# Start of a transformer-block kernel: the first loads spread over three queues, and the warming products on another operand

## The chip, the cores and the metric

The kernel runs on one core of one Trainium2 chip. The metric is the device time of one execution in microseconds (us). The kernel before took 763.39 us, the median of three runs that lie between 763.17 and 763.40 us. A core has five engines that run side by side and wait for each other through semaphores: TensorE (PE, with the weight loads as a track of their own, PEld), VectorE (DVE), ScalarE (ACT), GpSimd (POOL) and SyncE (SP). Transfers are issued from the queues of SP, ScalarE or GpSimd and carried by 16 DMA engines.

## The reference

One block of 512 positions and 1024 features: a gated linear attention and a latent attention in parallel, merged, then a squared-ReLU feed-forward, all in float32.

```python
def rmsnorm(x, g):
    xf = x.astype(jnp.float32)
    y = xf * lax.rsqrt(jnp.mean(xf * xf, axis=-1, keepdims=True) + EPS)
    return (y * g.astype(jnp.float32)).astype(x.dtype)

def reference(x, positions, g_mix, w_in, ...):
    h = x
    for l in range(DEPTH):
        n = rmsnorm(h, g_mix[l])
        proj = n @ w_in[l]
        (gq, gk, gv, gr, z_gf, z_gb, cq, ckv, kr, z_ma, z_mb) = jnp.split(proj, SPLIT_IDX, axis=-1)
        y_gla = gla_branch(gq, gk, gv, gr, z_gf, z_gb, ...)
        y_mla = mla_branch(cq, ckv, kr, positions, ...)
        merged = jax.nn.sigmoid(z_ma) * y_gla + jax.nn.sigmoid(z_mb) * y_mla
        h = h + merged @ w_out[l]
        m = rmsnorm(h, g_mlp[l])
        h = h + jnp.square(jax.nn.relu(m @ w_ff1[l])) @ w_ff2[l]
    return rmsnorm(h, g_final)
```

What matters here is the first line of the loop and the beginning of the second: x times the norm's factors g_mix, and its product with the first 512 columns that the kernel uses of w_in.

## The kernel before

Features lie on the 128 partitions and positions in the free dimension, so x comes transposed ("xt") in eight tiles of 128 features by 512 positions, xraw[0] to xraw[7] (256 KB each; called x in the profile). The first four blocks of output features that are projected have their weights gathered in "w_first", eight tiles of 128 by 512, vraw[0] to vraw[7] (256 KB each; vw in the profile). The factors of all norms, the biases and a few constants come in one array "columns" of 128 rows of 39 words, which lands in gvec; gmix is the part of it for the first norm.

A float32 product is made of three products of a narrower type: every operand is split into a high half (rounded) and a low half (the rest), and high times high, low times high and high times low are added up in one accumulator. So each tile costs ScalarE an activation for the high half and VectorE a subtraction for the low half before TensorE can use it. For x the high half carries the factors too (split_scaled, lines 97 and 98: ScalarE multiplies by gmix and rounds, VectorE multiplies and subtracts the rounded half). For the weights split does it (lines 93 and 94), except for the first tile: there VectorE makes the high half by a copy (line 341, CAST in the profile) and the low half by a subtraction (line 343). VectorE's order for this first tile is: high half of the weights, low half of x, low half of the weights.

first_with(k) (line 327) makes the twelve products of tile k: four accumulators f_accs (called first) by three pairs of halves, in the order high by high, low weights by high x, high weights by low x. In the profile the halves of the first two weight tiles are first0h and first0l, those of the next two first1h and first1l, and so on; xT is x's pair of halves.

What happens at the start, with the lines that the change and the prediction speak of:

- GpSimd builds ident (the unit matrix, by make_identity in masks.py), after (line 137 and 138), ones (line 142) and the small constants half_pi and mhalf. ident is used later for transposing and for diagonals (line 289), mhalf as the exponent of the reciprocal roots (line 279).
- VectorE copies ones into ones_r (line 144), the operand with which a diagonal is spread over the partitions (line 298).
- ScalarE loads its function table (line 150) and issues the transfer of gvec on its own queue (line 155).
- SP's queue issues x[0], vw[0], x[1], vw[1] and so on (lines 311 and 312), then the weights of later stages, in the order of the program. A transfer that reuses one of eight semaphores waits on the queue until the earlier transfer of that semaphore has landed.
- TensorE makes eight warming products ident times ident into an accumulator that nobody reads (line 317; 16 records in the profile, two passes for each product), and then the products of line 327.

The order of the work on each engine from line 315 on is the order of the program: in_program_order(fixed) adds a dependency without a semaphore from each instruction to the next of its engine. goes_behind(late, early, engines) does the same for one pair: the first instruction of `late` on an engine comes after the last one of `early` there. Lines further down (from line 355) multiply xraw by gmix in place, sum the squares, and project the next blocks (zb2, zb3), whose weights are transferred by begin_late (line 238).

```python
for k in range(KD):
    nc.sync.dma_start(xraw[k], t["xt"][k * P : (k + 1) * P, :])
    nc.sync.dma_start(vraw[k], t["w_first"][k * P : (k + 1) * P, :])
...
for _ in range(8):
    nc.tensor.matmul(warm[:, :P], ident, ident, start=True, stop=True)
```

Of the kernel before, what the change touches and what calls it, by code (L numbers as in the profile page):

```python
# [11 lines left out]
F32 = mybir.dt.float32  # L12
# [6 lines left out]
P = 128  # L19
# [37 lines left out]
def tile_block(ctx: ExitStack, tc: tile.TileContext, t, out: bass.AP):  # L57
    nc = tc.nc
# [9 lines left out]
    def u2(name, dt=F32, shape=(P, S)):  # L68
        return tl(list(shape), dt, "u2", 29, name)
# [7 lines left out]
    def ps(tag, name):  # L77
        serial[0] += 1
        return pp.tile([P, S], F32, tag=tag, bufs=4, name=f"{name}_{serial[0]}")

    def one(shape, dt, name):
        return sb.tile(shape, dt, tag=name, bufs=1, name=name)

    def raw(x):
        return x.bitcast(F32)
# [14 lines left out]
    def issued_after(ins, before):  # L100
        tc.add_manual_dep(
            ins, before,
            mybir.DependencyInfo(mybir.DependencyClass.NoSync, mybir.DependencyReason.DATA),
            reason="program order",
        )

    def traced():
        return len(nc.cur_bb.bb.instructions)
# [12 lines left out]
    SP_ONLY = (mybir.EngineType.SP,)  # L121
# [3 lines left out]
    def goes_behind(late, early, engines):  # L125

        ins = nc.cur_bb.bb.instructions
        for e in engines:
            a, b = [[i for i in ins[x:y] if i.engine == e] for x, y in (early, late)]
            if a and b:  # L130
                issued_after(b[0], a[-1].name)


    ident = one([P, P], F32, "ident")
    make_identity(nc, ident)
    after = one([P, P], F32, "after")
# [2 lines left out]
        after, after, pattern=[[-1, P]], compare_op=ALU.is_gt, fill=0.0, base=0, channel_multiplier=1  # L139
    )  # L140
    ones = one([P, P], F32, "ones")
    nc.gpsimd.memset(ones, 1.0)
    ones_r = one([P, P], F32R, "ones_r")
    nc.vector.tensor_copy(ones_r, ones)
    half_pi = one([P, 1], F32, "half_pi")
# [4 lines left out]
    nc.scalar.preload_act_table_set("exp_and_others")  # L150


    V_GLA, V_Q, V_KV, V_MLP, V_BF, V_BB, V_MIX, V_CST = 0, 8, 11, 13, 21, 25, 29, 37
    gvec = one([P, 48], F32, "gvec")
    nc.scalar.dma_start(gvec[:, 0 : V_CST + 2], t["columns"])
    gmix, cst = gvec[:, V_MIX : V_MIX + 8], gvec[:, V_CST : V_CST + 2]

    gates = {}
# [52 lines left out]
    def stage(nk, nw, name):  # L211
        wf = tl([P, nk, nw], F32, "wf", 3, f"{name}f")
        return wf

    def halves(nk, nw, name):
        wh = tl([P, nk, nw], F32R, "wh", 4, f"{name}h")
        wl = tl([P, nk, nw], F32R, "wl", 4, f"{name}l")
        return wh, wl
# [16 lines left out]
    def begin_late(col, name, tag="mm", w=None):  # L235

        wf = stage(KD, P, name)
        nc.sync.dma_start(wf, (w_in if w is None else w)[:, col : col + P].rearrange("(k p) w -> p k w", p=P))
        wh, wl = halves(KD, P, name)
        nc.scalar.activation(wh, wf, AF.Copy)  # L240

        def lows():
            nc.vector.tensor_tensor(wl, wf, raw(wh), op=ALU.subtract)

        return (wh, wl, ps(tag, name)), lows
# [20 lines left out]
    def feature_sums(sq, name, tag="at"):  # L266
        tot = ps(tag, f"{name}ss")
        for j in range(NT):
            nc.tensor.matmul(tot[:, j : j + 1], sq[:, j * P : (j + 1) * P], ones[:, 0:1], start=True, stop=True)
        return tot  # L270
# [36 lines left out]
    xraw = [u2(f"x{k}") for k in range(KD)]  # L307
    vraw = [u2(f"vw{k}") for k in range(KD)]

    for k in range(KD):  # L310
        nc.sync.dma_start(xraw[k], t["xt"][k * P : (k + 1) * P, :])
        nc.sync.dma_start(vraw[k], t["w_first"][k * P : (k + 1) * P, :])

    fixed = traced()
    warm = ps("at", "warm")
    for _ in range(8):
        nc.tensor.matmul(warm[:, :P], ident, ident, start=True, stop=True)
    f_accs = [ps("mm", f"first{i}") for i in range(NT)]
    vh = [halves(2, S, f"first{k}") for k in range(KD // 2)]
    sq = None  # L320
# [10 lines left out]
    def add_square(k, before):  # L331
        q = u2(f"sq{k}")
        nc.scalar.activation(q, xraw[k], AF.Square)
        if before is not None:
            nc.vector.tensor_tensor(q, q, before, op=ALU.add)
        return q
# [13 lines left out]
            sq = add_square(k - 1, sq)  # L350
    sq = add_square(KD - 1, sq)
    x_tot = feature_sums(sq, "x")
    zb_early = [begin_late(C_ZB + f * P, f"zb{f}", tag) for f, tag in ((2, "at"), (3, "mm"))]
    for k in range(KD):
        nc.scalar.activation(xraw[k], xraw[k], AF.Copy, scale=gmix[:, k : k + 1])
    first_with(6)
# [756 lines left out]
    for n, (a, m) in enumerate(steps[:-4]):  # L1113
# [4 lines left out]
        if steps[n + 1] in fillers:  # L1118
            at = traced()
# [113 lines left out]
    at = traced()  # L1233
# [8 lines left out]
    at = traced()  # L1242
# [8 lines left out]
    at = traced()  # L1251
# [12 lines left out]
    for n in range(4 * MH + LAG_C - 1):  # L1264
# [43 lines left out]
        if n == 17:  # L1308
            at = traced()
# [246 lines left out]
    at = traced()  # L1556
# [9 lines left out]
    at = traced()  # L1566
# [7 lines left out]
    at = traced()  # L1574
# [12 lines left out]
    at = traced()  # L1587
# [55 lines left out]
def build(arrays):  # L1643
    nc = bacc.Bacc("TRN2", target_bir_lowering=False, num_devices=1, dynamic_dma_scratch_size=8192)
    t = {
        n: nc.dram_tensor(f"in_{n}", list(a.shape), mybir.dt.from_np(a.dtype), kind="ExternalInput").ap()
        for n, a in arrays.items()
    }
    out = nc.dram_tensor("out_0", [1, S, D], F32, kind="ExternalOutput").ap()
    with tile.TileContext(nc) as tc:  # L1650
        tile_block(tc, t, out)
    return nc
# [16 lines left out]
```

## Time and profile before

| | before |
|---|---|
| median of 3 runs | 763.39 us |
| all runs | 763.39, 763.17, 763.40 us |
| the profiled execution's own time | 762.79 us |
| its span, first to last instruction | 761.0 us |
| mean granted TensorE clock | 0.999 |
| transfers | 81.28 MB, mean 107 GB/s |

The profile shows one execution. Its page gives busy time and share for each engine, the span in 40 slices, the transfers, and the chain of work that ended last, followed back from the end. The other views are answers from the same trace: a timeline (start, duration, engine with the line of the source, operation, output<-inputs, shapes, count, and in brackets the idle time of the engine before the instruction and what ended it), busy times in windows, and the instructions of one tile or one line. "x<-in_xt" is a transfer into a tile x from the input xt. SPq, ACTq and POOL mark the queue that issues a transfer; the time beside it is that of issuing, and the time to landing is shown apart. Times start at the first instruction of the span. The end of a matmul is modelled, so that the start of one is the better mark.

### The profile page before, as it was taken

Reading aid. Unit: us, or ns where it says so; the run is one execution under the profiler, and the core shown is the slowest. Engines: PE = TensorE matmul, PEld = TensorE weight load, DVE = VectorE, ACT = ScalarE, POOL = GpSimd, SP = SyncE. Lnnn points to the kernel's source line nnn. Section 1 sums busy time; section 2 is a strip of 40 time slices with the busy share of each in tenths; the row PEclk is TensorE's granted clock in tenths of the full one; section 3 lists DMA queues with packets and bytes.
Section 4 is the critical chain, followed back from the end, with each engine's and each line's share of the span. In section 5 each row is a group of like instructions: output and inputs, shape, how many; then the busy total and the mean of one; then the engine's idle time right before and its main releaser. Section 6 shows DMA issues by size and latency. Waiting matters only on the chain.

```text
span 761.0 us, 10233 instructions
## 1 busy us (share of the span) xinstructions
PE 752.1 (99%) x3744; PEld 636.1 (84%) x3744; DVE 580.7 (76%) x850; ACT 453.3 (60%) x768; POOL 150.5 (20%) x226
## 2 busy tenths in 40 slices
PE   9999999999999999999999999999999999999996
PEld 7888788888898889898888988888888888888885
DVE  7779999756767775998897786955796578748795
ACT  8456668475466555888866675435553555345644
POOL 0710005260615104127761100000000000000014
PEclk9999999999999999999999999999999999999999
DMA  9843310221324416127988421362116410650002
GB/s 312 255 112 108 93 28 28 56 59 54 84 60 112 82 33 155 25 71 191 272 189 229 140 80 56 111 196 80 55 56 195 137 42 15 195 165 1 28 1 110
DMA packets 97185, 81.28 MB, mean 107 GB/s; under 512 B 15504, under 2 KB 74896, under 8 KB 97136
## 3 DMA queue, kind: packets, MB, share of 16 engines
q1 hardware_dynamic: 93904, 74.33, 33.3%
q0 software_dynamic: 2944, 6.03, 4.3%
q8 instruction: 29, 0.48, 0.3%
q10 hardware_dynamic: 288, 0.28, 0.1%
q14 instruction: 20, 0.16, 0.1%
HBM read 76.96 MB, written 2.10 MB: 104 GB/s over the span
## 4 chain that ended last, share of the span: by engine, by line
PE 97%; DVE 1%; ACT 1%; issue 0%; POOL 0%; POOLq 0%; ACTq 0%
PE f L88 8%; PE f L89 8%; PE f L90 8%; PE gx L88 4%; PE gx L90 4%; PE gx L89 4%; PE first L327 3%; PE tp L1042 2%; PE za L88 2%; PE za L89 2%; PE za L90 2%; PE gz L88 2%; PE gz L90 2%; PE gz L89 2%; PE zb L88 1%; PE zb L90 1%
## 5 line engine op out<-in xcount | busy, mean ns | idle before, releaser
L1608 POOL DMA_DIRECT2D gfin<-in_g_final x1 | 0.6, 622 | 284.0 <-PE f L90 284.0
L914 DVE TENSOR_TENSOR w<-w,w 128x1024 f32<-128x1024 f32 x32 | 38.7, 1221 | 0.3
L475 POOL COPY v3f<-rrf 128x4 f32<-128x4 f32 x4 | 2.8, 708 | 135.9 <-DVE rrf L458 135.9
L1027 ACT ACTIVATE e<-s,top 128x512 f32<-128x512 f32 x32 | 21.9, 685 | 4.8 <-DVE top L1022 3.9
L94 DVE TENSOR_TENSOR pT<-tp,pT 128x512 fp32r<-128x512 f32 x32 | 21.7, 682 | 2.9 <-ACT pT L93 2.9
L1022 DVE TENSOR_REDUCE top<-s 128x1 f32<-128x512 f32 x32 | 21.6, 681 | 2.0 <-PE s L90 1.7
L1335 DVE TENSOR_TENSOR h<-h,gx 128x512 f32<-128x512 f32 x32 | 21.5, 682 | 1.9 <-PE gx L90 1.8
L93 ACT ACTIVATE pT<-tp 128x512 fp32r<-128x512 f32 x32 | 18.8, 593 | 4.2 <-PE tp L1042 3.9
L1042 PE MATMUL tp<-ident,e 128*128 128x128 f32 x128 | 19.3, 274 | 0.4 <-ACT e L1033 0.2
L88 PE MATMUL av<-pT,v 128*128 128x256 f32 x64 | 19.0, 297 | 0.0
L93 ACT ACTIVATE ghb<-y 128x512 fp32r<-128x512 f32 x16 | 10.1, 632 | 14.0 <-DVE y L860 14.0
L1401 ACT ACTIVATE fa<-f 128x512 f32<-128x512 f32 x32 | 18.5, 577 | 0.0
L89 PE MATMUL av<-pT,v 128*128 128x256 f32 x64 | 18.2, 285 | 0.0
L1042 PEld LDWEIGHTS tp<-ident,e 128*128 128x128 f32 x128 | 15.1, 140 | 3.7 <-ACT e L1033 1.0
L94 DVE TENSOR_TENSOR sc<-sc,sc 128x512 fp32r<-128x512 f32 x16 | 10.9, 691 | 9.5 <-ACT sc L93 9.5
L90 PE MATMUL av<-pT,v 128*128 128x256 f32 x64 | 18.1, 283 | 0.0
L93 ACT ACTIVATE sc<-sc 128x512 fp32r<-128x512 f32 x16 | 9.3, 596 | 11.5 <-DVE sc L546 11.5
L93 ACT ACTIVATE b_00h<-w 128x1024 fp32r<-128x1024 f32 x7 | 7.4, 1061 | 12.6 <-PE gx L90 6.0
L93 ACT ACTIVATE b_20h<-w 128x1024 fp32r<-128x1024 f32 x7 | 7.4, 1061 | 12.1 <-PE gx L90 6.0
L93 ACT ACTIVATE b_10h<-w 128x1024 fp32r<-128x1024 f32 x7 | 7.4, 1061 | 12.1 <-PE gx L90 6.0
L88 PE MATMUL s<-kbuf,q 96*128 96x512 f32 x32 | 14.1, 440 | 0.0
L1410 ACT ACTIVATE px<-fa 128x256 f32<-128x256 f32 x32 | 13.4, 418 | 1.0
(1667 smaller groups left out, 2927.9 us busy)
## 6 DMA issues: line engine op xcount, KB each, us to landing
w<-in_w_ff SPq DMA_DIRECT2D x64, 256.0 KB, 3.5
w<-in_w_out POOLq DMA_DIRECT2D x10, 512.0 KB, 9.4
grw<-in_w_in SPq DMA_DIRECT2D x8, 512.0 KB, 8.5
gvw<-in_w_in SPq DMA_DIRECT2D x8, 512.0 KB, 4.6
w<-in_w_out SPq DMA_DIRECT2D x16, 256.0 KB, 5.8
x<-in_xt SPq DMA_DIRECT2D x8, 256.0 KB, 5.2
vw<-in_w_first SPq DMA_DIRECT2D x8, 256.0 KB, 5.3
h<-in_x SPq DMA_DIRECT2D x4, 512.0 KB, 5.0
```

What stands on the lines that cost most here:

```text
L88: nc.tensor.matmul(acc, lh, rh, start=start, stop=False, skip_group_check=onto)
L89: nc.tensor.matmul(acc, lh, rl, start=False, stop=False, skip_group_check=onto)
L90: nc.tensor.matmul(acc, ll, rh, start=False, stop=stop, skip_group_check=onto)
L93: nc.scalar.activation(hi, src, AF.Copy)
L94: rest.tensor_tensor(lo, src, raw(hi), op=ALU.subtract)
L327: nc.tensor.matmul(f_accs[i], a[:, i * P : (i + 1) * P], b, start=k == 0 and x == 0, stop=k == KD - 1 and x == 2)
L914: nc.vector.tensor_tensor(wq[dst][g], wq[x][g], wq[y][g], op=op)
L1022: nc.vector.tensor_reduce(top, acc, axis=AX.X, op=ALU.max, negate=True)
L1027: nc.scalar.activation(e, acc, AF.Exp, bias=top, accum_out=tot[:, qt % 2 : qt % 2 + 1])
L1042: nc.tensor.transpose(tp[:, k * P : (k + 1) * P], e[:, k * P : (k + 1) * P], ident)
L1335: nc.vector.tensor_tensor(hc, hc, acc, op=op)
L1401: nc.scalar.activation(a, acc, AF.Relu)
```

## The change

Four things at the start of the program are changed; nothing is added to or taken from the computation.

1. The transfer of gvec moves from ScalarE's queue to GpSimd's and stands ahead of everything else there.
2. The transfer of the first weight tile, vw[0], moves from SP's queue to ScalarE's. The other weight tiles and all of x stay on SP's.
3. ones is filled by VectorE in place of GpSimd, and the eight warming products take ones for both operands in place of ident.
4. The transfers of zb2 and zb3 are tied behind those of x and w_first on SP's queue by goes_behind.

```diff
+    V_GLA, V_Q, V_KV, V_MLP, V_BF, V_BB, V_MIX, V_CST = 0, 8, 11, 13, 21, 25, 29, 37
+    gvec = one([P, 48], F32, "gvec")
+    nc.gpsimd.dma_start(gvec[:, 0 : V_CST + 2], t["columns"])
     ident = one([P, P], F32, "ident")
     make_identity(nc, ident)
...
     ones = one([P, P], F32, "ones")
-    nc.gpsimd.memset(ones, 1.0)
+    nc.vector.memset(ones, 1.0)
     ones_r = one([P, P], F32R, "ones_r")
     nc.vector.tensor_copy(ones_r, ones)
...
-    V_GLA, V_Q, V_KV, V_MLP, V_BF, V_BB, V_MIX, V_CST = 0, 8, 11, 13, 21, 25, 29, 37
-    gvec = one([P, 48], F32, "gvec")
-    nc.scalar.dma_start(gvec[:, 0 : V_CST + 2], t["columns"])
     gmix, cst = gvec[:, V_MIX : V_MIX + 8], gvec[:, V_CST : V_CST + 2]
...
+    landing = traced()
     for k in range(KD):
         nc.sync.dma_start(xraw[k], t["xt"][k * P : (k + 1) * P, :])
-        nc.sync.dma_start(vraw[k], t["w_first"][k * P : (k + 1) * P, :])
-
+        (nc.sync if k else nc.scalar).dma_start(vraw[k], t["w_first"][k * P : (k + 1) * P, :])
+
+    landing = landing, traced()
     fixed = traced()
     warm = ps("at", "warm")
     for _ in range(8):
-        nc.tensor.matmul(warm[:, :P], ident, ident, start=True, stop=True)
+        nc.tensor.matmul(warm[:, :P], ones, ones, start=True, stop=True)
...
     x_tot = feature_sums(sq, "x")
+    at = traced()
     zb_early = [begin_late(C_ZB + f * P, f"zb{f}", tag) for f, tag in ((2, "at"), (3, "mm"))]
+    goes_behind((at, traced()), landing, SP_ONLY)
```

In the program as built, the order on each engine is the one of before except for these: VectorE begins with the memset of ones and the copy into ones_r (before, that copy stood after the low half of the second weight tile), GpSimd begins with the transfer and no longer fills ones, and SP's queue has one transfer less, so that x[1] follows x[0] there. zb2 and zb3 stood behind x and w_first before, too.

## The prediction

> **What bounds the kernel now.** I read the page's shares first, then the chain of work that ended last, then the first microseconds by timeline, windows and tiles, because every edit lies there.
>
> ```profile
> span 761.0 us, 10233 instructions
> PE 752.1 (99%) x3744; PEld 636.1 (84%) x3744; DVE 580.7 (76%) x850; ACT 453.3 (60%) x768; POOL 150.5 (20%) x226
> 1.53 3.50 PE warm L317 x16
> 5.03 0.96 PE first L327 x4
> 6.01 15.71 PE first L327 x68
> ```
>
> TensorE is busy 752.1 of 761.0 us. The chain starts with the warming products and goes straight into the first projections; from 6.01 on they run without a gap (68 products in 15.71 us, 0.231 each). So the moment at which TensorE enters that unbroken run carries to the end one for one, and nothing earlier counts. What sets 6.01 is in the timeline (start, duration, engine, work, then the idle time before it and what ended that):
>
> ```profile
> 0.80 0.39 SPq L311 DMA_DIRECT2D x<-in_xt  x1
> 0.82 0.39 ACTq L155 DMA_DIRECT2D gvec<-in_columns  x1
> 1.18 0.29 POOL masks.py:199 TENSOR_SCALAR_AFFINE_SELECT ident<-ident 128x128 f32<-128x128 f32 x1
> 1.24 0.42 SPq L312 DMA_DIRECT2D vw<-in_w_first  x1
> 1.53 3.31 PEld L317 LDWEIGHTS warm<-ident 128*128 128x128 f32 x16 [1.53 <-POOL ident masks.py:199]
> 1.68 0.20 POOL L142 MEMSET ones<- 128x128 f32 x1
> 1.70 0.43 SPq L311 DMA_DIRECT2D x<-in_xt  x1
> 3.84 0.72 ACT L97 ACTIVATE xT<-x,gvec 128x512 fp32r<-128x512 f32 x1 [1.77 <-DMA gvec<-in_columns]
> 4.26 0.43 DVE L341 CAST first0h<-vw 128x512 fp32r<-128x512 f32 x1 [4.26 <-DMA vw<-in_w_first]
> 4.60 0.75 DVE L98 SCALAR_TENSOR_TENSOR xT<-x,gvec,xT 128x512 fp32r<-128x512 f32 x1
> 4.80 0.75 PEld L327 LDWEIGHTS first<-xT,first0h 128*128 128x128 f32 x4
> 5.27 0.68 DVE L343 TENSOR_TENSOR first0l<-vw,first0h 128x512 fp32r<-128x512 f32 x1
> 5.64 0.72 ACT L97 ACTIVATE xT<-x,gvec 128x512 fp32r<-128x512 f32 x1 [1.07 <-DMA x<-in_xt]
> 6.00 0.76 PEld L327 LDWEIGHTS first<-xT,first0l 128*128 128x128 f32 x4 [0.46 <-DVE first0l L343]
> 6.28 0.63 ACT L93 ACTIVATE first0h<-vw 128x512 fp32r<-128x512 f32 x1
> 7.07 0.69 DVE L94 TENSOR_TENSOR first0l<-vw,first0h 128x512 fp32r<-128x512 f32 x1
> 7.67 0.22 DVE L144 CAST ones_r<-ones 128x128 fp32r<-128x128 f32 x1
> ```
>
> Read backwards: the second group of products (6.00) waits 0.46 us for the low half of the first weights (DVE, 5.27 to 5.95). That follows on VectorE the low half of x (4.60 to 5.35), and that has two predecessors which end together. One is ScalarE's high half of x, 3.84 to 4.56, waiting for the norms' factors; the other is VectorE's own cast of the first weights, which waits for their tile and starts at 4.26, so that the next instruction follows 0.34 later. Thus
>
> low half of x starts = the later of (ScalarE start + 0.76) and (cast start + 0.34): 4.60 and 4.60,
>
> and TensorE's unbroken run starts 1.40 later. Both arms are tight: a gain needs both earlier, a loss needs only one later. The warming products are a third arm for the first group alone (4.80), which is followed by the 0.46 us gap and so has that much slack.
>
> How long the transfers take from issue to landing (views by line or by tile: the issue's row, then minimum, median and maximum of that row's transfers):
>
> ```profile
> L155 ACTq DMA_DIRECT2D gvec<-in_columns x1: 394/394/394, 0.8 to 0.8; - x1
> DMA to landing us min/median/max: 2.9/2.9/2.9
> L311 SPq DMA_DIRECT2D x<-in_xt x3: 388/432/432, 0.8 to 2.7; - x3
> DMA to landing us min/median/max: 2.7/3.9/4.3
> L312 SPq DMA_DIRECT2D vw<-in_w_first x2: 416/424/433, 1.2 to 2.2; - x2
> DMA to landing us min/median/max: 3.0/3.5/4.1
> L1129 POOL DMA_DIRECT2D pos_i<-in_positions x1: 772/772/772, 41.0 to 41.0; - x1
> DMA to landing us min/median/max: 3.8/3.8/3.8
> ```
>
> The shortest x is the first (an empty queue): it lands at 0.80 + 2.7 = 3.5. The first weight tile lands at 1.24 + 3.0 = 4.2, the factors at 0.82 + 2.9 = 3.7, which is 0.1 before ScalarE starts. The last pair of rows is GpSimd's first transfer today, 256 KB, at 41 us.
>
> **The change, part by part.** The order of instructions on each engine stays the same but for the moved ones.
>
> *First weight tile on ScalarE's queue.* Issued at 0.82 in place of 1.24, so at best it lands at 0.82 + 2.7 (the first x) = 3.5, 0.7 earlier; at worst at 4.2 as now. Which, the windows say (length, busy times, granted clock, DMA share, GB/s):
>
> ```profile
> 1.50:2.00 0.50, 0.47 (x2) 0.47 (x3) 0.00 (x0) 0.50 (x1) 0.50 (x6) 1.00 0.87 61
> 2.00:2.50 0.50, 0.50 (x4) 0.50 (x4) 0.00 (x0) 0.07 (x1) 0.02 (x1) 1.00 0.36 124
> 2.50:3.00 0.50, 0.50 (x5) 0.50 (x4) 0.00 (x0) 0.00 (x0) 0.00 (x0) 1.00 1.04 371
> 3.00:3.50 0.50, 0.50 (x4) 0.50 (x4) 0.00 (x0) 0.00 (x0) 0.00 (x0) 1.00 1.06 385
> 3.50:4.00 0.50, 0.50 (x4) 0.50 (x4) 0.00 (x0) 0.16 (x1) 0.00 (x0) 1.00 1.14 324
> ```
>
> From 2.5 us on the transfer engines are full. In the first two windows they move 31 + 62 = 93 KB, then 186 and 193 KB. The first x (262 KB) and the factors (20 KB, 128 rows of 39 words) make 282 KB, done at 3.0; with the weight tile 544 KB, done at 3.7. Each lands about 0.5 later, which fits 3.5 and 4.2. Nothing is idle that an earlier issue could use, except before 2.5. If the weight tile's packets take turns with x from 2.5 on, x has some 170 KB left and gets half of 380 GB/s: done 0.9 later, at 3.4, landing at 3.9 instead of 3.5. Bounds: x lands at 3.5 (it keeps its place) to 4.2 (both end together); the weights at 3.5 to 4.2. I take 3.9 for x and 4.1 for the weights, since a second queue's transfer (the factors today) already lands beside the first x and not behind the transfers queued on SP. The second x is issued 0.46 earlier (at 1.24), but the bytes ahead of it are the same 512 KB, so ScalarE's second high half stays near 5.64. It may be late by some 0.9: it ends, with its weights, at 6.28 + 0.63 = 6.91, and TensorE needs it only after twelve products, 6.0 + 8 x 0.231 = 7.8.
>
> The Trainium skill ("DMA: Bandwidth & Descriptors", section "Issuing engines are not separate DMA queues") says that transfers issued from several engines interleave on the same 16 DMA engines and that only issue time is saved. By it the sum's gain would be at most the 0.42 us of issue time in the weights' arm, while x pays for the interleaving; the full windows above agree with it.
>
> *Factors on GpSimd.* Issued at about 0.79, before its first memset. Bounds for the landing: 2.9 as on ScalarE's queue (3.7), and 3.8 as for the positions (4.6). The positions carry 256 KB, which at 380 GB/s is 0.7 us; without them 3.1, or 3.9. But they landed on idle engines, and the factors have to take turns with two streams where they now have one. I take the middle of the bounds, 4.1. GpSimd's other start work is delayed by the issue, 0.77 as for the positions. Its cover is in these rows (the power reads mhalf, the diagonal reads ident), ident, for one, is written at 1.18:
>
> ```profile
> 22.86 1.89 POOL L279 TENSOR_TENSOR r_x<-r_x,mhalf 128x4 f32<-128x4 f32 x1 [20.84 <-DVE r_x L278]
> 25.60 1.23 DVE L289 TENSOR_TENSOR xdg<-ident,xrh 128x512 fp32r<-128x512 f32 x1
> ```
>
> Without that cover it would cost its 0.77.
>
> *Warming operand on VectorE.* VectorE stands idle until 4.26, so the memset (0.20 on GpSimd; on VectorE between half and twice the 0.22 of the cast, which has the same shape) and the cast, moved from 7.67, are free there. The warming products start at about 0.79 + 0.20 + 0.06 = 1.05, 0.48 earlier, and are through by about 4.3. They did not set 6.00, so this gives nothing; the removed 0.22 at 7.67 lies in VectorE's slack (the second tile's low weights, just ahead of it, are ready at 7.76 and needed after 7.8 + 4 products = 8.7). Order constraints on the SP queue: nothing.
>
> *Sum.* ScalarE starts at 4.1 + 0.1 = 4.2 (factors; x at 3.9 is earlier), the low half of x at 4.2 + 0.76 = 4.96 (weights' arm 4.1 + 0.37 = 4.47), against 4.60: +0.35. Between the two estimates of the landing, 3.9 and 4.1, it is +0.15 to +0.35; I round to +0.3. Profiled execution: 762.79 = span 761.0 + 1.8 around it, so 763.1; the median of the runs, 763.39, lies 0.6 above the profiled one, so 763.7. Bounds: all at the early ends gives ScalarE at 3.6 or 3.8, so -0.2 to 0; the factors at 4.6 give +0.9.
>
> **Rivals.**
>
> *It does what it says* (25%). The factors land as before or earlier, x keeps its place, the weights gain 0.4. For it: GpSimd has nothing before the issue, and 20 KB is little. Against it: the full windows. ScalarE at 3.6 to 3.8: 763.2 to 763.4.
>
> *The factors come much too late* (5%; slower). One transfer from GpSimd, made under full queues, behaves like its later ones beside SP's stream:
>
> ```profile
> L910 POOL DMA_DIRECT2D w<-in_w_out x10: 1181/1248/1692, 355.7 to 400.5; - x10
> DMA to landing us min/median/max: 5.9/9.4/12.6
> ```
>
> Even the quickest of them, 5.9, puts the landing at 6.7 and ScalarE at 6.8, 3.0 later: 766.4. It decides from a landing at 5.3 (4.5 after the issue), where the loss passes 1.5 us. Against it: those move 512 KB each and add to what lies there; the positions took 3.8.
>
> *The clock is late* (3%; slower).
>
> ```profile
> L317 PEld LDWEIGHTS warm<-ident x16: 192/333/333, 1.5 to 4.6; 128*128 128x128 f32 x16
> ```
>
> The warming loads run at 333 ns and the last at 192, some 3.1 us after the first: TensorE comes to speed just as the products begin. If the earlier warming ends at 4.3, TensorE rests until 5.2, and another 3.1 us from 4.3 has to pass, the products up to 7.4 take twice as long: half of 2.2, 1.1, with the 0.3 above 764.8. Against it: warming starts earlier too and should reach speed by 4.2. The Trainium skill ("TensorE: Matmul & The Clock Gate", section "What's actually happening") has free-running windows of 3413 ns, by which the step could also come up to a window later; no run here shows that.
>
> **How the numbers follow.** The forecast (+0.1 to +0.9, mostly by the factors or x) holds 67%, the gain 25%, late factors 5%, late clock 3%. What a measurement of this kernel can tell from no change is about 0.2%, 1.5 us. The gain and the forecast both lie within it; beyond it on the slow side lie late factors and a small part of the rest, 6%; on the fast side there is no room, since both arms end in transfers that cannot land before 3.5, so 1%. The range is 763.0 (the gain, with the spread of the runs) to 764.5 (factors at 4.6 and 0.2 of spread).
>
> **What would show it.** In the changed profile ScalarE's first high half should start at 4.0 to 4.4 and name gvec or x as its releaser, the first cast at or a little before 4.2, the warming products near 1.05, and TensorE's second group near 6.3 after a gap on the low weights. The forecast is wrong if ScalarE starts before 3.84, if the second group starts before 6.0, if TensorE has a new gap between 6.3 and 30 us, or if the clock step comes after the first products.

## The result, and the profile after

| | before | after |
|---|---|---|
| median of 7 runs on one chip | 763.40 us (762.90 to 764.05) | 766.38 us (765.53 to 766.65) |
| ratio, 95% interval | | 1.0035 (1.0023 to 1.0047) |
| the profiled execution's own time | 762.79 us | 765.86 us |
| its span | 761.0 us | 764.1 us |

The change makes the kernel 2.98 us slower by the medians (1.8 to 3.6 by the interval), which is outside the predicted range and more than the 0.2% that a measurement of this kernel can tell from no change. The page of the changed kernel still has TensorE as the bound, busy 99% of a span that is 3.1 us longer. 1.9 of these 3.1 us are more busy time (754.0 against 752.1), and that is the first hint that waiting alone does not explain the loss (a product at a slow clock is busy for longer):

```profile
span 764.1 us, 10232 instructions
PE 754.0 (99%) x3744; PEld 637.5 (83%) x3744; DVE 580.7 (76%) x851; ACT 453.1 (59%) x768; POOL 151.1 (20%) x226
```

The chain of waits after no longer begins with the warming products. Its first links (start, duration, work) are the factors' transfer, ScalarE's high half of x, and then TensorE without a gap:

```profile
1.33 4.31 DMA gvec<-in_columns
5.67 0.73 ACT xT L97
6.44 17.97 PE first L329 x72
```

The timeline after, in the columns of the timeline before:

```profile
0.82 0.40 ACTq L313 DMA_DIRECT2D vw<-in_w_first  x1
1.11 3.49 PEld L319 LDWEIGHTS warm<-ones 128*128 128x128 f32 x16 [1.11 <-DVE ones L145]
1.33 0.76 POOL L136 DMA_DIRECT2D gvec<-in_columns  x1 [0.83 <-POOLq L1648]
4.76 0.43 DVE L343 CAST first0h<-vw 128x512 fp32r<-128x512 f32 x1 [3.44 <-DMA vw<-in_w_first]
5.67 1.33 ACT L97 ACTIVATE xT<-x,gvec 128x512 fp32r<-128x512 f32 x2 [3.59 <-DMA gvec<-in_columns]
6.42 0.75 DVE L98 SCALAR_TENSOR_TENSOR xT<-x,gvec,xT 128x512 fp32r<-128x512 f32 x1 [1.23 <-ACT xT L97]
6.44 1.35 PEld L329 LDWEIGHTS first<-xT,first0h 128*128 128x128 f32 x4 [1.84 <-ACT xT L97]
7.89 1.57 PEld L329 LDWEIGHTS first<-xT,first0l 128*128 128x128 f32 x4
9.49 1.79 PEld L329 LDWEIGHTS first<-xT,first0h 128*128 128x128 f32 x8
```

Beside it, the third group of products in the timeline before:

```profile
6.80 1.80 PEld L327 LDWEIGHTS first<-xT,first0h 128*128 128x128 f32 x8
```

Read the starts one after the other. ScalarE begins 1.83 us late (5.67 against 3.84), because the factors were issued at 1.33 and took 4.3 us. TensorE's second group is 1.89 late (7.89 against 6.00). The third group is 2.69 late (9.49 against 6.80): another 0.80 was lost between the second and the third group, where TensorE waits for nobody. The durations say why. Four loads of the first group take 1.35 us where they took 0.75, and those of the second 1.57 where they took 0.76: these eight products ran at the slow pace of the warming. The record of TensorE's granted clock that each trace keeps (no view prints its events) says the same: the clock goes up to full at 9.36 us, in the trace before at 4.60. After that the two traces run in step. The gate's activations, one row of each kernel's view by tile (minimum, median and maximum duration in ns, first and last start), are 2.7 and 2.6 us apart; before:

```profile
L442 ACT ACTIVATE l<-gatef,gvec x4: 682/684/692, 111.1 to 216.6; 128x512 f32<-128x512 f32 x4
```

and after:

```profile
L446 ACT ACTIVATE l<-gatef,gvec x4: 683/684/691, 113.8 to 219.2; 128x512 f32<-128x512 f32 x4
```

The remaining 0.4 us of the span (3.1 less 2.69) come somewhere later. Executions of the kernel before differ by more than that among themselves, so it is not pursued. The account is 1.8 us for late factors, 0.8 us for slow first products.

Issue and landing after, by tile (the issue's row, then minimum, median and maximum from issue to landing; for a line with several issues the first is the shortest):

```profile
L136 POOL DMA_DIRECT2D gvec<-in_columns x1: 757/757/757, 1.3 to 1.3; - x1
DMA to landing us min/median/max: 4.3/4.3/4.3
L312 SPq DMA_DIRECT2D x<-in_xt x8: 328/393/519, 0.8 to 8.5; - x8
DMA to landing us min/median/max: 3.8/5.3/5.7
L319 PEld LDWEIGHTS warm<-ones x16: 288/333/337, 1.1 to 4.3; 128*128 128x128 f32 x16
```

The first x lands at 0.80 + 3.8 = 4.6 and the weight tile just before its cast, at 4.7. Both are later than the prediction's worst case of 4.2, only the factors are later still. The last row shows that the warming never came to speed: none of its sixteen loads took less than 288 ns, where the last one before took 192.

### The profile page after: what moved, and what is told of

Read it like the earlier page. It is cut to its first block, busy times and chain, and to the rows that moved or that the text cites. A ratio compares the mean times of both kernels' runs of the same rounds, so it can differ in the third digit from the quotient of the medians.

```text
span 764.1 us, 10232 instructions
## 1 busy us (share of the span) xinstructions
PE 754.0 (99%) x3744; PEld 637.5 (83%) x3744; DVE 580.7 (76%) x851; ACT 453.1 (59%) x768; POOL 151.1 (20%) x226
## 4 chain that ended last, share of the span: by engine, by line
PE 96%; DVE 1%; ACT 1%; DMA 1%; issue 0%; POOL 0%; POOLq 0%; ACTq 0%
PE f L88 8%; PE f L90 8%; PE f L89 8%; PE gx L88 4%; PE gx L89 4%; PE gx L90 4%; PE first L329 3%; PE tp L1046 2%; PE za L88 2%; PE za L89 2%; PE za L90 2%; PE gz L90 2%; PE gz L88 2%; PE gz L89 2%; PE zb L88 1%; PE zb L89 1%
```

## The experiments

The question was which of the moved pieces costs the 1.8 us, whether the 0.8 us is TensorE's clock, and why 20 KB take 4.3 us from GpSimd. The kernel before ran on the same chip beside each: its median was 763.60 us beside the first four experiments, 763.40 beside the held stream, the two repeats and the last kernel of all, and 763.44 beside the others. Ratios are to these.

**Factors back on ScalarE's queue, ahead of the weight tile.** Taken from the changed kernel:

```diff
-    nc.gpsimd.dma_start(gvec[:, 0 : V_CST + 2], t["columns"])
+    nc.scalar.dma_start(gvec[:, 0 : V_CST + 2], t["columns"])
```

> The changed kernel with the factors back on ScalarE's queue, ahead of the first weight tile there; SP carries x and the other weight tiles as in the change. Theory 'GpSimd's path': the factors land near 3.9, and only the smaller loss from the two queues taking turns stays: x lands near 4.5, ScalarE starts near 4.6 (3.84 before, 5.67 changed), the time is 0.8 to 1.2 us over before, 1.8 to 2.2 us under the change. Rival 'two queues' (the interleaving of x and the first weight tile is the whole cause, and delayed the factors too): ScalarE starts above 5.2 and the time stays within 0.7 us of the change. Rival 'nothing but GpSimd': ScalarE starts by 3.9 and the time is that of before.

Measured: median 766.12 us, ratio 1.0027 (1.0016 to 1.0039), with six runs in two groups: 764.23 and 764.57, and four from 765.79 to 766.56. The profile is that of the 764.23. Its timeline:

```profile
1.26 0.43 ACTq L313 DMA_DIRECT2D vw<-in_w_first  x1
3.89 0.72 ACT L97 ACTIVATE xT<-x,gvec 128x512 fp32r<-128x512 f32 x1 [1.38 <-DMA gvec<-in_columns]
5.05 0.43 DVE L343 CAST first0h<-vw 128x512 fp32r<-128x512 f32 x1 [3.73 <-DMA vw<-in_w_first]
6.80 0.76 PEld L329 LDWEIGHTS first<-xT,first0l 128*128 128x128 f32 x4 [0.44 <-DVE first0l L345]
7.61 1.79 PEld L329 LDWEIGHTS first<-xT,first0h 128*128 128x128 f32 x8
```

ScalarE is back at 3.89, so the 1.8 us by which it was late belonged to the factors. But the weights' arm is now late. Their tile, issued at 1.26 (1.24 before), lands 3.8 later (3.0 before), the cast starts at 5.05 instead of 4.26, and the third group is 0.81 late. This is about the expected size for an execution whose products run at speed, but not at the expected place: x was to land near 4.5, and it landed at 3.7, while the weights were late. The median missed it, and why there are two groups was left to later runs, below.

**Weight tile back on SP's queue, factors still on GpSimd.**

```diff
-        (nc.sync if k else nc.scalar).dma_start(vraw[k], t["w_first"][k * P : (k + 1) * P, :])
+        nc.sync.dma_start(vraw[k], t["w_first"][k * P : (k + 1) * P, :])
```

> The changed kernel with the first weight tile back on SP's queue; the factors stay on GpSimd as its first work. Theory 'GpSimd's path': the factors are issued near 1.33 and land at 5.2 to 5.7, though x lands near 3.5 again; ScalarE starts at 5.3 to 5.7 and the time is 1.5 to 3 us over before. Rival 'two queues': with one queue at the start the factors land within 3 us of their issue, by 4.3, ScalarE starts by 4.4 and the time is at most 0.6 us over before.

Measured: median 766.39, ratio 1.0034 (1.0021 to 1.0046), the whole loss of the change. The timeline has the cast early again and the factors as late as ever:

```profile
4.13 0.43 DVE L343 CAST first0h<-vw 128x512 fp32r<-128x512 f32 x1 [2.82 <-DMA vw<-in_w_first]
5.78 1.34 ACT L97 ACTIVATE xT<-x,gvec 128x512 fp32r<-128x512 f32 x2 [3.71 <-DMA gvec<-in_columns]
```

The two queues are not needed for the loss; the factors from GpSimd are enough. The weight tile's move is enough for most of it too, by the median of the first experiment: 766.12 with that move alone, 766.39 with the factors' alone, 766.38 with both. The two losses do not add up; the part on the clock, below, gives a reading of why.

**The warming operand alone,** on the kernel before: ones filled by VectorE, the warming products on ones.

```diff
-    nc.gpsimd.memset(ones, 1.0)
+    nc.vector.memset(ones, 1.0)
...
-        nc.tensor.matmul(warm[:, :P], ident, ident, start=True, stop=True)
+        nc.tensor.matmul(warm[:, :P], ones, ones, start=True, stop=True)
```

> The kernel before with ones filled by VectorE and the warming products on ones; all transfers as before. Theory: ScalarE still starts near 3.84 and TensorE's second group near 6.0; warming runs from 1.1 to 4.5 to 4.9 and there is no gap ahead of the first products, so the time is that of before within 0.4 us. Rival 'clock': the earlier warming ends before TensorE's speed comes up, the first products' weight loads run at 333 ns in place of 188, and the time is 0.8 us or more over before.

Measured: median 763.64, ratio 1.0001 (0.9992 to 1.0010). This part costs nothing that can be measured. Against this kernel, the second experiment's differs in the queue of the factors (and in part 4 of the change, which left the order on SP's queue as it was): 763.64 and 766.39 beside the same kernel before.

**Twice the warming,** on the changed kernel, so that TensorE works until the late first products come:

```diff
-    for _ in range(8):
+    for _ in range(16):
```

> The changed kernel with sixteen warming products in place of eight. Theory: the gap of 1.55 us ahead of the first products goes, the weight loads of the first eight products run at 188 ns in place of 333, TensorE's third group starts 0.7 to 0.9 us earlier (near 8.7), and the time is 0.5 to 1.0 us under the change; the rest of the loss, about 2 us over before, stays because ScalarE still starts near 5.6. If the slow first products had another cause than the gap, nothing changes, or the longer warming itself delays the first products (later than 6.5).

Measured: median 765.11, ratio 1.0022 (1.0013 to 1.0031). Timeline:

```profile
1.11 5.01 PEld L319 LDWEIGHTS warm<-ones 128*128 128x128 f32 x32 [1.11 <-DVE ones L145]
5.52 1.33 ACT L97 ACTIVATE xT<-x,gvec 128x512 fp32r<-128x512 f32 x2 [3.45 <-DMA gvec<-in_columns]
6.29 0.76 PEld L329 LDWEIGHTS first<-xT,first0h 128*128 128x128 f32 x4 [0.17 <-ACT xT L97]
7.68 0.75 PEld L329 LDWEIGHTS first<-xT,first0l 128*128 128x128 f32 x4 [0.63 <-DVE first0l L345]
8.48 1.81 PEld L329 LDWEIGHTS first<-xT,first0h 128*128 128x128 f32 x8
```

Here all products run at speed (four loads in 0.76 and 0.75), and the third group comes at 8.48 instead of 9.49. ScalarE was 0.15 earlier here, so 0.8 to 0.9 of that is the slow pace taken away. What stays over before is 1.68 us in the trace (8.48 less 6.80) and 1.51 by the medians, less than the 2 that were expected: the factors' share. That the longer warming is what took the slow pace away is not shown by this one trace, since its clock goes up at 4.01 us, which eight products would have reached as well. The times speak for it: seven of the ten lie from 764.93 to 765.23, under all twelve of the two kernels with late factors and eight warming products (765.41 to 766.79).

**Where GpSimd's time goes: a spare transfer late in the kernel.** On the kernel before, 8 KB that nobody reads, once while SP streams weights and once right behind the positions, when SP's queue moves nothing (gvec's tile is narrowed to make room):

```diff
+    spare = one([P, 16], F32, "spare")
+    nc.gpsimd.dma_start(spare, t["columns"][:, 0:16])
...
+            nc.gpsimd.dma_start(spare, t["columns"][:, 0:16])
```

> The kernel before with two more small transfers from GpSimd, 128 rows of 16 words into a tile that nobody reads: one at about 25 us, where the DMA engines are full with SP's stream, one at about 42 us, where they are nearly idle. It asks where the 4.3 us of the factors come from. If from full engines: the first lands 4 us or more after its issue, the second in 2 to 3. If from the first use of GpSimd's queue in the program or from the start of the kernel: both land in 2 to 3 us, or the first alone is longer but under 3.5.

Measured in one execution: 763.1 us. By tile, and the DMA share of both places in windows (length, busy times, granted clock, DMA share, GB/s):

```profile
L360 POOL DMA_DIRECT2D spare<-in_columns x1: 771/771/771, 24.8 to 24.8; - x1
L1132 POOL DMA_DIRECT2D spare<-in_columns x1: 534/534/534, 44.5 to 44.5; - x1
DMA to landing us min/median/max: 3.5/4.8/6.1
```

```profile
24.00:26.00 2.00, 2.00 (x11) 1.63 (x10) 1.12 (x3) 0.51 (x1) 1.97 (x3) 1.00 1.03 383
43.00:45.00 2.00, 2.00 (x10) 1.66 (x9) 0.35 (x2) 1.58 (x2) 1.99 (x5) 1.00 0.00 0
```

The first one, on full engines (share 1.03), is the one that took 6.1 us; the second, on engines that were idle up to its issue (share 0.00) and then carried the positions' 256 KB, took 3.5, which is above the 2 to 3 that was expected. The same 8 KB cost 2.6 us more in the first place. This need not all be the crowd: GpSimd went on computing right behind the first issue and had nothing to do behind the second, and the first transfer's packets start only 4.2 us after the issue and are through 0.6 us later. The run does not part the two.

**A spare transfer as GpSimd's first work,** with the factors on ScalarE's queue as before and the warming operand of the change:

```diff
+    spare = one([P, 16], F32, "spare")
+    nc.gpsimd.dma_start(spare, t["columns"][:, 0:16])
     ident = one([P, P], F32, "ident")
```

> The kernel before with the warming operand of the change, the factors on ScalarE's queue as before, and one small transfer that nobody reads (128 rows of 16 words) as GpSimd's first work. It asks whether the transfer from GpSimd costs by itself (its issue, its delay of ident) or only because ScalarE waits for it. Theory: it is issued near 1.33 and lands near 5.5, as the factors do in the change, ScalarE starts at 3.8 to 4.0, and the time is that of before within 0.5 us. Rival: its presence delays x or the weights and the time is 1 us or more over before.

Measured: median 763.23, ratio 0.9997 (0.9988 to 1.0006).

```profile
1.31 0.76 POOL L135 DMA_DIRECT2D spare<-in_columns  x1 [0.82 <-POOLq L1646]
```

It starts as late as the factors did (1.31) and lands 4.5 us later, but costs nothing that can be measured: the transfer costs only through who waits for it, and GpSimd's constants have their cover.

**The stream held back,** to see whether the engines' load is what makes 4.4 out of 3: the kernel of the second experiment, with SP's queue stopped behind the first x and the first weights until the factors have landed:

```diff
+        if k == 0:
+            nc.sync.dma_start(spare, gvec[:, 0:16])
+    in_program_order(landing, SP_ONLY)
```

> The factors on GpSimd, x and all weights on SP, and SP's queue held behind the first x and the first weight tile until the factors have landed (a transfer out of gvec stands third on it). Only 512 KB are then under way beside the factors. If the factors' 4.3 to 4.4 us come from the full DMA engines, they land 2.5 to 3.3 us after their issue, near 4.2, and ScalarE starts near 4.3 in place of 5.7. If they come from GpSimd's path itself or from the start of the kernel, the landing stays above 4 us. The time will be worse than the change's in either case, since everything behind on SP starts late.

Measured in one execution: 776.1 us, since the whole stream is late. Its start:

```profile
1.33 0.76 POOL L136 DMA_DIRECT2D gvec<-in_columns  x1 [0.83 <-POOLq L1652]
4.33 0.56 SPq L316 DMA_DIRECT2D spare<-gvec  x1
4.34 0.72 ACT L97 ACTIVATE xT<-x,gvec 128x512 fp32r<-128x512 f32 x1 [2.27 <-DMA gvec<-in_columns]
```

Issued at the same 1.33, the factors now land at 4.33: 3.0 us instead of 4.4. So 1.4 us of the transfer is the stream beside it. The packets of GpSimd's queue (q0) in the two traces show where it goes; by windows (packets that start there, MB, share of the engines), with the stream held, from 3.48 to 4:

```profile
q0 software_dynamic: 32, 0.02, 12.5%
```

and in the second experiment, from 3.5 to 4:

```profile
q0 software_dynamic: 25, 0.02, 44.0%
```

In both the first packet starts at about 3.5, 2.2 us after the issue, so the stream costs nothing up to there. With the stream held, all 32 are through at 3.98. Beside it, seven start only after 4.0, three of the 32 take more than 1 us each, and the last ends at 5.43.

**The first kernel again, twice.** Exactly the first experiment's kernel, executed once more each, to see what parts its two groups of times:

> The same kernel as with the factors on ScalarE's queue ahead of the first weight tile, whose times fell into two groups (764.2 to 764.6, and 765.8 to 766.6) and whose profile was of the lower one. A look for one of the upper group: by the theory of the clock its first products load weights at 333 ns for some 3 us after their start, with the transfers as they were (ScalarE at 3.9, first cast near 5.0); by the theory of the transfers x or the weights land later by 1.5 us or more.

> Once more the same, for the same question: a profile of the upper group shows slow first products (clock) or late transfers.

Measured: 764.57 and 766.26. The timeline of the first:

```profile
4.26 0.72 ACT L97 ACTIVATE xT<-x,gvec 128x512 fp32r<-128x512 f32 x1 [1.74 <-DMA gvec<-in_columns]
5.41 0.43 DVE L343 CAST first0h<-vw 128x512 fp32r<-128x512 f32 x1 [4.09 <-DMA vw<-in_w_first]
5.95 0.76 PEld L329 LDWEIGHTS first<-xT,first0h 128*128 128x128 f32 x4 [1.35 <-ACT xT L97]
9.79 0.87 PEld L329 LDWEIGHTS first<-xT,first0l 128*128 128x128 f32 x4
```

and of the second:

```profile
4.04 1.55 ACT L97 ACTIVATE xT<-x,gvec 128x512 fp32r<-128x512 f32 x2 [1.52 <-DMA gvec<-in_columns]
5.20 0.43 DVE L343 CAST first0h<-vw 128x512 fp32r<-128x512 f32 x1 [3.88 <-DMA vw<-in_w_first]
5.74 1.35 PEld L329 LDWEIGHTS first<-xT,first0h 128*128 128x128 f32 x4 [1.15 <-ACT xT L97]
8.90 2.54 PEld L329 LDWEIGHTS first<-xT,first0h 128*128 128x128 f32 x8
11.48 0.88 PEld L329 LDWEIGHTS first<-xT,first0l 128*128 128x128 f32 x4
```

In the second, the factors and the first weight tile landed about 0.2 us *earlier*, and yet the group at 11.48 comes 1.69 later than its twin at 9.79, exactly the difference of the two times. Its first four loads take 1.35 us instead of 0.76, and its loads come to speed only in the group that starts at 8.90. The clock records put the step at 4.65 and at 10.46. So the two groups of times are TensorE's step to full speed, which can fall at another moment in each execution of one program.

**Factors on ScalarE's queue and twice the warming,** the first and fourth experiments together.

> The changed kernel with the factors back on ScalarE's queue ahead of the first weight tile, and sixteen warming products. The same without the longer warming had times in two groups, 764.2 to 764.6 and 765.8 to 766.6. Theory 'clock': the upper group is TensorE running slowly after the gap; with the gap filled all runs lie near 764.4, within 0.6 us of each other, 0.6 to 1.2 us over before (what the first weight tile on a second queue costs by itself). Rival: the two groups come from the transfers, and stay.

Measured: median 765.14, ratio 1.0023 (1.0015 to 1.0032), eleven runs from 764.47 to 765.90. The narrow group near 764.4 that was expected did not come. In the timeline, of an execution of 764.66, the first products start at 6.33, though their cast starts at 5.11:

```profile
6.33 0.77 PEld L329 LDWEIGHTS first<-xT,first0h 128*128 128x128 f32 x4
```

Its loads follow the warming with no wait. In the first experiment they started 0.55 us after the cast; here sixteen warming products are still running when the operands are there: warming that is too long delays what it was to help. That also hides the factors in the medians: 765.14 here, 765.11 where they are late (twice the warming on the changed kernel), with first products at 6.33 and 6.29; the third groups still tell the two apart, 8.05 against 8.48. The spread of 1.4 us would fit a step that comes sooner or later and so makes the sixteen products shorter or longer, but only one of these executions has a trace.

**Two attempts to beat the kernel before.** Its 0.46 us gap ahead of the second group goes away if high weights by low x comes second. Once alone, and once with the warming operand of the change:

```diff
-        for x, (a, b) in enumerate(((wh, hi), (wl, hi), (wh, lo))):
+        for x, (a, b) in enumerate(((wh, hi), (wh, lo), (wl, hi))):
```

> The kernel before, with the twelve products of a tile in the order high by high, high weights by low x, low weights by high x. If the start is set by VectorE's order (high weights, low x, low weights) as the prediction's formula has it, TensorE's second group waits for the low half of x (ready at 5.35) in place of the low weights (5.95), and starts right behind the first, near 5.74 in place of 6.00: 0.2 to 0.4 us under before. If the formula is wrong, no change.

> The kernel before with both of the parts that cost nothing so far: the products in the order high by high, high weights by low x, low weights by high x, and the warming on ones that VectorE fills. TensorE's second group follows the first without a gap; 0.2 to 0.6 us under before (the first part alone had a median 0.47 under it, with an interval that holds no change). If the lower median was chance, the time is that of before.

Measured: medians 762.97, ratio 0.9995 (0.9986 to 1.0004), and 763.05, ratio 0.9996 (0.9987 to 1.0005). The timeline of the first has the gap gone:

```profile
4.90 1.88 PEld L327 LDWEIGHTS first<-xT,first0h 128*128 128x128 f32 x8
6.83 0.88 PEld L327 LDWEIGHTS first<-xT,first0l 128*128 128x128 f32 x4
```

Eight loads without a break, but they start 0.1 later than before and some are slow (1.88 us for eight where the row at 6.80 above has 1.80), so that the third group, at 6.83, is where it was. Both medians lie 0.35 to 0.47 us under the kernel before, and both intervals hold no change. No version is shown to beat it.

## Why the prediction was wrong

**The step that failed is the landing of the factors.** The prediction has them "issued at about 0.79" and takes for the landing "the middle of the bounds, 4.1", with 4.6 as the upper bound. They were issued at 1.33 and landed at 5.63. Two terms were wrong:

- The issue, by 0.54. The 0.79 is the start of the memset that stood first on GpSimd before; a transfer in that place starts at 1.31 to 1.33 in each kernel that has one. The profile puts the wait down to GpSimd's own sequencer (POOLq), and before had no transfer there that could have shown it.
- The landing, 4.3 after the issue against an estimate of 3.3. The prediction's upper bound of 3.8 was read from the positions' transfer at 41 us. It said itself that "they landed on idle engines", and yet used the row as an upper bound, while its own windows had the engines full from 2.5 us on. A row taken without load is a lower bound for the same transfer under load. Measured, the factors took 3.0 us with the stream held back and 4.4 with it, in two kernels that differ in the hold alone (and in the width of gvec's tile).

ScalarE's queue carries the same 20 KB in 2.9 to 3.4 us, but at another moment: its first packet starts 1.2 to 1.7 us after an issue at 0.8, between 2.0 and 2.5, when the stream is only building up. GpSimd's, issued at 1.33, start at 3.5 at the earliest and, in the changed kernel, at 4.31. Why this last 0.8 us came on top, and why a few packets then take so long, is open. The Trainium skill ("DMA: Bandwidth & Descriptors", section "SWDGE vs HWDGE vs iDMA") states that each DMA engine takes turns between its queues and that GpSimd's transfers feed other queues than SP's and ScalarE's. That alone would give a small transfer its turn early. The first packet of the second experiment agrees with it (3.5, as with the stream held); the 1.4 us that are lost behind that packet do not, and no run shows what the three slow packets wait for.

**A rival that happened, at the wrong price.** "The factors come much too late" was priced from GpSimd's transfers beside SP's stream, the right row, and given 5% because these move 512 KB and because "the positions took 3.8". That argument preferred size over load; the held stream says that load is worth 1.4 us to 20 KB. The mechanism happened with a landing at 5.63, between the 5.3 from which it was said to decide and the 6.7 of its price. That its 766.4 us meet the measured 766.38 is luck: the factors brought 1.8 of its 3.0 us, and the slow products, which this rival leaves out, 0.8.

**A second rival came with it.** "The clock is late" was given 3% as something apart. But the factors' lateness is what makes the rest between the end of the warming (4.89) and the first product (6.44), and eight products then ran at the slow pace: 0.8 us, against the 1.1 priced. The clock step came after the first products, which is one of the prediction's own signs of being wrong. Twice the warming closes the rest, and its times are lower. That "warming starts earlier too and should reach speed by 4.2" was wrong: all sixteen loads are slow, as they are in each kernel that starts eight warming products at 1.1. Before, 3.1 us of warming brought speed; here 3.5 us from 1.11 did not. The Trainium skill ("TensorE: Matmul & The Clock Gate", section "What's actually happening") says that the activity window runs free and does not begin with the kernel. The two executions of one program agree with that: one ran at speed from its first group of products, the other only within its third.

The clock records of the fourteen traces allow a closer reading. In each of them the time at full clock is a whole multiple of 3.413 us (in the trace before 754.345 us, 221 times as long). Cut the time ahead of the rise into pieces of the same length: in the last piece, which ends with the rise, TensorE was busy for 2.9 us or more in every trace, and in none of the earlier pieces for more than 2.53 (the ends of products are modelled, so these are not exact). By this reading a rest of 0.9 us can spoil a piece, and the rise then waits for the end of the next, 3.4 us later; where the pieces begin differs from execution to execution, so whether a rest does harm is luck. In the twelve executions of the two kernels with late factors and eight warming products, where TensorE rests for 1.6 us in both traces, the time was never below 765.4. With the factors on ScalarE's queue it rests for 0.7 to 1.1 in the three traces, and three of eight executions were in the quick group. This reading would explain why either move alone costs about as much as both: each makes a rest in which the rise may be lost.

**What held.** TensorE's start carried to the end about one for one. The formula held on both arms: 5.67 + 0.76 = 6.43 against 6.42 in the changed kernel, and in the first experiment the cast's 5.05 + 0.34 + 1.40 = 6.79 against 6.80. The order on the engines was as foretold, the warming started at 1.11 against 1.05, and the new operand and GpSimd's delayed constants cost nothing that can be measured.

**Right in sign, too small, and hidden.** "I take 3.9 for x and 4.1 for the weights", with 4.2 as the worst for both; they landed at 4.6 and 4.7. In the windows the engines came up more slowly than before, when they moved 61, 124 and 371 GB/s in these three half microseconds (278 KB in all, here 203):

```profile
1.50:2.00 0.50, 0.50 (x4) 0.50 (x4) 0.00 (x0) 0.50 (x1) 0.50 (x1) 1.00 0.14 8
2.00:2.50 0.50, 0.50 (x4) 0.50 (x4) 0.00 (x0) 0.07 (x1) 0.48 (x4) 1.00 0.78 180
2.50:3.00 0.50, 0.50 (x5) 0.50 (x4) 0.00 (x0) 0.00 (x0) 0.50 (x3) 1.00 0.98 217
```

Here the late factors cover this. Without them, in the first experiment, the weight tile's place on another queue cost 0.8 us by itself: beside SP's stream it may share the engines with the second x, which on SP's queue stands behind it. That the sharing, and not another effect of the queue, is the cause was not tried by itself.

## What to carry to other kernels

Price a transfer from a row with the same issuing queue and the same load on the DMA engines; a row from an idle stretch bounds it from below only, and a small transfer can take as long as a large one there (8 KB took 6.1 us beside the stream, the quickest 512 KB 5.9). The small transfer that everything at the start waits for belongs on the queue that answers first, here ScalarE's. Warming products should last until the first real product and not much longer, so anything that delays that product is priced together with the clock, not beside it: here a rest of about one microsecond could cost 1.7.

## What the hardware showed that was not expected

- A transfer as GpSimd's first work starts 0.5 us later than a memset in the same place (1.33 against 0.79), and takes 4.2 to 4.5 us to land at this kernel's start and 3.0 there with the stream held, for 8 to 20 KB. Later in the kernel 8 KB took 3.5 us behind the positions, and 6.1 beside the full weight stream with GpSimd itself at work. The Trainium skill ("DMA: Bandwidth & Descriptors", section "Anatomy of one DMA — SWDGE (gpsimd) path") has a fit for GpSimd's transfers, 2.0 us plus the bytes at 436 GB/s, by which 20 KB would take 2.05 us, as an estimate; all measured ones lie above it, counted from the start of the issue.
- The granted clock in the windows reads 1.00 while the loads run at 333 ns instead of 188. The traces' clock records begin only with the rise (at 4.60 us before, 9.36 after), and the column counts the time ahead of it as full, so the duration of the loads is what shows the slow pace at the start.
- One program can take its step to full speed at another moment in each execution (4.65 and 10.46 us), which is worth up to 1.7 us where TensorE rests ahead of the first products.
